# Loads issued by GpSimd instead of SyncE in a row-wise largest-magnitude kernel

## The chip, the cores and the metric

The kernel runs on one core of one Trainium2 chip. A core has several engines with instruction streams of their own: VectorE (DVE), ScalarE (ACT), GpSimd (POOL), TensorE (PE, not used here) and SyncE (SP), which has no arithmetic and issues transfers. Sixteen DMA engines move data between HBM and the on-chip memory SBUF, which has 128 partitions. The metric is the device time of one execution in microseconds. The profile of the kernel before has a span of 625.7 us from its first to its last record, for an execution of 627.43 us.

## The reference

For each row of an 8192 x 8192 matrix of 32-bit floats, the largest absolute value:

```python
def setup_inputs():
    return {"x": np.random.randn(8192, 8192).astype(np.float32)}

def reference(x):
    return np.linalg.norm(x, ord=np.inf, axis=1)
```

Each element is read once and only 8192 numbers are written. There is 268.44 MB to load and 0.03 MB to store.

## The kernel before

The rows are dealt to the 128 partitions so that each partition holds a run of neighbouring rows, 46 in the first group and 18 in the second. A "column" of 8192 elements is then one row of the matrix in every partition, and 64 columns make the whole. Loads are two columns wide (16384 elements, 64 KB in each partition) but for the first two and the last ones. They go into a ring in SBUF that holds three of the wide ones.

```python
GROUPS = [46, 18]
WHOLE = (
    [(8192, ())] * 2 + [(16384, ())] * 29 + [(16384, (3712, 3680)), (8192, (2016, 1984))]
)
LAST = [
    (3920, (1680,)), (1984, (848,)), (1040, (432,)), (576, (240,)), (320, ()), (352, ())
]
RING = 3 * 16384
```

Each entry is the width of a load and, in the inner brackets, what VectorE leaves to ScalarE and GpSimd of its last column: ScalarE makes it absolute, GpSimd takes the maximum. Without inner brackets VectorE reduces it all. The loads:

```python
    def load(pos, w):
        # ... cut: the place in the ring, `at`; the last load has a tile of its own
            buf = ring[:, at : at + w]
        inst = nc.sync.dma_start(out=buf, in_=x_of[first[row]][:, a : a + w]).ins
        # ... cut: for half of the loads, the dependency on the earlier load
        #     of the same place is dropped: the reduce in between orders them
        return buf
```

A load may start when the reduce of what stood in its place is done. The main loop, and the end:

```python
    pos = 0
    for u, (w, g) in enumerate(WHOLE):
        buf = load(pos, w)
        # ... cut
        if whole:
            red = absmax(res[:, row : row + whole], buf[...])     # VectorE
        if g:
            part = single.tile([P, 1 + len(g)], FP32, name=f"part{u}")
            shared(part, buf[:, whole * n_cols :], g)   # VectorE, and ScalarE then GpSimd
            max_pool(res[:, row + whole : row + k], part)         # GpSimd
        # ... cut: an early activation that loads ScalarE's table

    for h, (w, g) in enumerate(LAST[:-1]):
        buf = load(pos, w)
        pos += w
        shared(last[:, n : n + 1 + len(g)], buf, g)
        n += 1 + len(g)

    load(pos, LAST[-1][0])
    absmax(res[:, R - 1 :], last)
    final = nc.sync.dma_start(out=out_of[first[-1]][:, GROUPS[-1] - 1 :], in_=res[:, R - 1 :])
    # ... cut: two earlier stores, issued by ScalarE
```

Line 68 of the kernel is VectorE's reduce, line 75 GpSimd's, line 90 ScalarE's activation, line 108 the load, lines 154 and 159 the stores.

Of the kernel before, what the change touches and what calls it, by code (L numbers as in the profile page):

```python
# [1 line left out]

# [4 lines left out]

P = 128
FP32 = mybir.dt.float32
INT32 = mybir.dt.int32  # L10
MAX = mybir.AluOpType.max
X = mybir.AxisListType.X
ABS = mybir.ActivationFunctionType.Abs
# [16 lines that stand above are left out]
@with_exitstack  # L30
def kernel(
    ctx: ExitStack,
    tc: tile.TileContext,
    x: bass.AP,
    out: bass.AP,
):
    nc = tc.nc
    n_rows, n_cols = x.shape
    R = n_rows // P
    assert R == sum(GROUPS) and n_cols == 8192  # L40
    keep = tc.keep_in_program_order


    first = []
    x_of, out_of = {}, {}
    for k in GROUPS:
        f = len(first)
        x_of[f] = x[f * P : (f + k) * P].rearrange("(p r) m -> p (r m)", r=k)
        out_of[f] = out[f * P : (f + k) * P].rearrange("(p r) -> p r", r=k)
        first += [f] * k  # L50

    single = ctx.enter_context(tc.tile_pool(name="single", bufs=1))

    ring = single.tile([P, RING], FP32)
    res = single.tile([P, R], FP32)

    n_parts = sum(1 + len(g) for w, g in LAST[:-1])
    last = single.tile([P, LAST[-1][0] + n_parts], FP32)

    def not_before(inst, other, why):  # L60
        tc.add_manual_dep(
            inst.ins, other.ins.name,
            mybir.DependencyInfo(mybir.DependencyClass.Sync, mybir.DependencyReason.DATA),
            reason=why,
        )

    def absmax(dst, src):
        return keep(nc.vector.tensor_reduce(  # L68
            out=dst, in_=src, axis=X, op=MAX, apply_absolute_value=True,
        ))  # L70

    def max_pool(dst, src):

        pool = nc.gpsimd
        keep(pool.add_instruction(  # L75
            mybir.InstTensorReduce(
                name=nc.get_next_instruction_name(),
                ins=[pool.lower_ap(src.bitcast(INT32))],
                outs=[pool.lower_ap(dst.bitcast(INT32))],
                op=MAX,  # L80
                axis=X,
            )
        ))

    def shared(part, buf, g):

        a = buf.shape[1] - sum(g)
        red = absmax(part[:, :1], buf[:, :a])
        for i, c in enumerate(g):
            keep(nc.scalar.activation(buf[:, a : a + c], buf[:, a : a + c], ABS))  # L90
            max_pool(part[:, 1 + i : 2 + i], buf[:, a : a + c])
            a += c
        return red

    loads = []

    def load(pos, w):

        row = pos // n_cols
        a = pos - first[row] * n_cols  # L100
        if pos + w == R * n_cols:
            buf = last[:, :w]
        else:
            at = loads[-1][0] + loads[-1][1] if loads else 0
            if at + w > RING:
                at = 0
            buf = ring[:, at : at + w]
        inst = nc.sync.dma_start(out=buf, in_=x_of[first[row]][:, a : a + w]).ins  # L108
        if pos + w < R * n_cols:
            if (len(loads) + 4) % 10 < 5:  # L110


                for b, v, earlier in loads:
                    if b < at + w and at < b + v:
                        tc.declare_no_dep(
                            inst, earlier, reason="ordered by the reduces in between",
                        )
            loads.append((at, w, inst))
        return buf


    pos = 0
    for u, (w, g) in enumerate(WHOLE):
        buf = load(pos, w)
        row, k = pos // n_cols, w // n_cols
        pos += w
        whole = k - 1 if g else k
        if whole:
            red = absmax(
                res[:, row : row + whole],  # L130
                buf[:, : whole * n_cols].rearrange("p (c m) -> p c m", m=n_cols),
            )
        if g:
            part = single.tile([P, 1 + len(g)], FP32, name=f"part{u}")
            shared(part, buf[:, whole * n_cols :], g)
            max_pool(res[:, row + whole : row + k], part)
        if u == 1:

            not_before(
                keep(nc.scalar.activation(res[:, :1], res[:, :1], ABS)),  # L140
                red, "not before the second row is in",
            )


    n = LAST[-1][0]
    for h, (w, g) in enumerate(LAST[:-1]):
        buf = load(pos, w)
        pos += w
        shared(last[:, n : n + 1 + len(g)], buf, g)
        n += 1 + len(g)  # L150

    load(pos, LAST[-1][0])
    absmax(res[:, R - 1 :], last)
    final = nc.sync.dma_start(out=out_of[first[-1]][:, GROUPS[-1] - 1 :], in_=res[:, R - 1 :])


    for f, o in out_of.items():
        k = min(o.shape[1], R - 1 - f)
        early = keep(nc.scalar.dma_start(out=o[:, :k], in_=res[:, f : f + k]))
        tc.add_manual_dep(  # L160
            early.ins, final.ins.name,
            mybir.DependencyInfo(
                mybir.DependencyClass.NoSync, mybir.DependencyReason.SCHED_ONLY
            ),
            reason="takes the later semaphore",
        )


# [1 line left out]
_INS = ['x']  # L170
_OUTS = [((8192,), 'float32')]


# [23 lines left out]
```

## Time and profile before

| What | Value |
|---|---|
| Time, median of 3 runs | 627.56 us (627.45 to 627.61) |
| Mean rate over the span | 429 GB/s |
| VectorE's reduce of 128 x 16384, each of 29 | 17.22 us |
| SyncE's issue of one load | 0.33 to 0.53 us |
| A wide load, issue to landing, median of 30 | 40.8 us |
| First wait of VectorE, for the first load | 12.85 us |

Times in the profile are us from the start of the span. SPq is SyncE's instruction stream, where issuing a load shows; a DMA entry runs from the issue to the landing of the data, so it holds the time in which the load stands behind others in the queue. The chain of waits goes back from the last instruction, at each step to what released it. The groups by line give for VectorE's wide and single reduces together 86.4 us of waiting, all of it for loads.

### The profile page before, as it was taken

How to read it: one execution, taken by the hardware profiler on the slowest of the kernel's cores; microseconds unless marked ns; L12 is line 12 of the kernel's file. 1: busy time of each engine (PE TensorE's matmuls, PEld its weight loads, DVE VectorE, ACT ScalarE, POOL GpSimd, SP SyncE). 2: the span in 40 equal slices, each digit the busy share in tenths (PEclk: the TensorE clock that was granted, in tenths of full speed). 3: DMA queues.
4: the chain of work that ended last, by engine and by line, in shares of the span. 5: the costliest groups of instructions: out<-in, count | busy, mean ns of one | idle time of the engine just before them, and what ended most of it. 6: DMA issues, size and time to landing. Idle time of an engine off the chain costs nothing.

```text
span 625.7 us, 175 instructions
## 1 busy us (share of the span) xinstructions
DVE 536.7 (86%) x40; ACT 15.1 (2%) x10; POOL 14.1 (2%) x14
## 2 busy tenths in 40 slices
DVE  1938988889888899888898888988889888899888
ACT  0000000000000000000000000000000000000044
POOL 0000000000000000000000000000000000000026
DMA  8999999999999999999999999999999999999997
GB/s 369 436 469 402 469 402 469 402 469 402 469 402 457 415 415 457 402 469 402 469 402 469 402 469 402 469 402 453 419 415 457 402 469 402 469 402 469 402 436 304
DMA packets 6048, 268.47 MB, mean 429 GB/s; under 512 B 1056, under 2 KB 1312, under 8 KB 1696
## 3 DMA queue, kind: packets, MB, share of 16 engines
q1 hardware_dynamic: 5760, 268.44, 99.3%
q10 hardware_dynamic: 288, 0.03, 0.0%
HBM read 268.44 MB, written 0.03 MB: 429 GB/s over the span
## 4 chain that ended last, share of the span: by engine, by line
DMA 71%; DVE 28%; SPq 0%; issue 0%; DVEq 0%
DMA ring<-in_x_dram 71%; DVE res L68 28%; DVE last L68 1%; SPq L108 0%; DVEq L68 0%
## 5 line engine op out<-in xcount | busy, mean ns | idle before, releaser
L68 DVE TENSOR_REDUCE res<-ring 128x2 f32<-128x16384 f32 (+1 forms) x32 | 525.4, 16420 | 86.4 <-DMA ring<-in_x_dram 86.4
L90 ACT ACTIVATE ring<-ring 128x3712 f32<-128x3712 f32 (+7 forms) x8 | 13.6, 1719 | 577.2 <-DMA ring<-in_x_dram 573.9
L75 POOL TENSOR_REDUCE part<-ring 128x1 int32<-128x3712 int32 (+3 forms) x4 | 10.1, 2562 | 607.6 <-ACT ring L90 607.6
L68 DVE TENSOR_REDUCE part<-ring 128x1 f32<-128x800 f32 (+1 forms) x2 | 5.5, 2748 | 0.1
L68 DVE TENSOR_REDUCE last<-ring 128x1 f32<-128x2240 f32 (+4 forms) x5 | 5.3, 1115 | 0.1
L75 POOL TENSOR_REDUCE last<-ring 128x1 int32<-128x1680 int32 (+3 forms) x4 | 3.4, 855 | 0.6 <-ACT ring L90 0.4
L140 ACT ACT_TABLE_LOAD x1 | 1.3, 1283 | 0.7 <-PEq L181 0.7
L140 ACT ACTIVATE res<-res 128x1 f32<-128x1 f32 x1 | 0.2, 203 | 29.3 <-DVE res L68 29.3
L68 DVE TENSOR_REDUCE res<-last 128x1 f32<-128x361 f32 x1 | 0.5, 529 | 0.1
L75 POOL TENSOR_REDUCE res<-part 128x1 int32<-128x3 int32 x2 | 0.4, 198 | 0.1
L181 POOL MEMSET const-float32-0.0<- 128x1 f32 x1 | 0.1, 99 | 0.2 <-issue 0.2
L181 POOL MEMSET const-bfloat16-1.0<- 128x1 bf16 x1 | 0.1, 102 | 0.0
L181 POOL MEMSET const-uint8-127<- 128x1 uint8 x1 | 0.1, 101 | 0.0
L181 POOL MEMSET const-float32-1.0<- 128x1 f32 x1 | 0.1, 99 | 0.0
## 6 DMA issues: line engine op xcount, KB each, us to landing
ring<-in_x_dram SPq DMA_DIRECT2D x3, 4096.0 KB, 21.4
ring<-in_x_dram SPq DMA_DIRECT2D x1, 1960.0 KB, 35.4
ring<-in_x_dram SPq DMA_DIRECT2D x1, 992.0 KB, 37.4
ring<-in_x_dram SPq DMA_DIRECT2D x1, 520.0 KB, 38.2
ring<-in_x_dram SPq DMA_DIRECT2D x30, 40.8
ring<-in_x_dram SPq DMA_DIRECT2D x1, 288.0 KB, 38.4
last<-in_x_dram SPq DMA_DIRECT2D x1, 176.0 KB, 38.3
ring<-in_x_dram SPq DMA_DIRECT2D x1, 160.0 KB, 38.3
```

Source lines behind the costliest of these rows:

```text
L68: return keep(nc.vector.tensor_reduce(out=dst, in_=src, axis=X, op=MAX, apply_absolute_value=True,))
L75: keep(pool.add_instruction(mybir.InstTensorReduce(name=nc.get_next_instruction_name(), ins=[pool.lower_ap(src.bitcast(INT32))], outs=[poo ...
L90: keep(nc.scalar.activation(buf[:, a : a + c], buf[:, a : a + c], ABS))
L140: keep(nc.scalar.activation(res[:, :1], res[:, :1], ABS)),
L181: nc = _bacc.Bacc("TRN2", target_bir_lowering=False, num_devices=1)
```

## The change

GpSimd issues every load instead of SyncE. GpSimd also has reduces of its own at the end of the kernel, and its stream is kept in program order, so a load that stood behind one of those reduces would come late. Therefore, as soon as the first shared column comes, all remaining loads are issued, and GpSimd's reduces follow them. The last store stays on SyncE. What is loaded, where to and in what order doesn't change, nor do the reduces. It tries the other way of starting a transfer: SyncE has its descriptors (the lists of what goes where) made by hardware, GpSimd makes them in software.

```diff
-        inst = nc.sync.dma_start(out=buf, in_=x_of[first[row]][:, a : a + w]).ins
+        inst = keep(nc.gpsimd.dma_start(out=buf, in_=x_of[first[row]][:, a : a + w])).ins
...
+    widths = [w for w, _ in WHOLE + LAST]
+    bufs = []
+
+    def load_up_to(n):
+        while len(bufs) < n:
+            bufs.append(load(sum(widths[: len(bufs)]), widths[len(bufs)]))
+
     pos = 0
     for u, (w, g) in enumerate(WHOLE):
-        buf = load(pos, w)
+        load_up_to(len(widths) if g else u + 1)
+        buf = bufs[u]
...
-    for h, (w, g) in enumerate(LAST[:-1]):
-        buf = load(pos, w)
-        pos += w
+    for buf, (w, g) in zip(bufs[len(WHOLE) :], LAST[:-1]):
         shared(last[:, n : n + 1 + len(g)], buf, g)
         n += 1 + len(g)
 
-    load(pos, LAST[-1][0])
     absmax(res[:, R - 1 :], last)
```

## The prediction

> **What bounds the kernel now.** I read the busy table first, then the DMA queues, the chain that ended last, a table of stretches, and a timeline of the end. By the page VectorE (DVE) is busy for 86% of the span and the DMA queue of the loads for over 99%:
>
> ```profile
> DVE 536.7 (86%) x40; ACT 15.1 (2%) x10; POOL 14.1 (2%) x14
> ...
> q1 hardware_dynamic: 5760, 268.44, 99.3%
> ```
>
> The second line is queue, packets, MB and share of sixteen DMA engines. The input is 8192 x 8192 x 4 bytes = 268.44 MB, so every byte is moved once. 39 loads and the last store, which shares SP's queue, make 5760 packets, 144 each: one for each of the 128 partition rows, and 16 short ones. A row of a two-column load is 16384 x 4 = 65,536 bytes, and it goes as one packet.
>
> The chain of waits shows how a round goes (start, length, what):
>
> ```profile
> 59.16 0.02 issue
> 59.17 40.78 DMA ring<-in_x_dram
> 99.95 0.02 issue
> 99.97 17.23 DVE res L68
> ...
> 564.39 17.23 DVE res L68
> 581.62 0.02 issue
> 581.64 0.33 SPq L108
> 581.97 0.05 issue
> 582.02 35.44 DMA ring<-in_x_dram
> 617.45 0.02 issue
> 617.47 5.30 DVE last L68 x5
> ```
>
> A reduce ends at 59.16, its third of the ring is free, the next load is issued at once and lands 40.78 us later. From 59.16 to 581.62 the chain makes nine such rounds of three loads each: 27 loads in 522.46 us, 19.35 us a load, and 8.389 MB / 19.35 us = 433.5 GB/s. A chain that alternates DMA and DVE looks like a latency loop. But of the 40.78 us only 19.35 are the load's own transfer; the other 21.43 are the loads queued ahead of it, and its issue and latency lie beside them. The table of stretches confirms that the queue doesn't run dry (stretch, length, busy DVE, ACT, POOL, clock, DMA share, GB/s):
>
> ```profile
> 59.17:117.22 58.05, 51.66 (x3) 0.00 (x0) 0.00 (x0) 1.00 1.00 434
> 117.22:291.37 174.15, 154.97 (x9) 0.00 (x0) 0.00 (x0) 1.00 1.00 434
> 291.37:581.64 290.27, 258.30 (x15) 0.00 (x0) 0.00 (x0) 1.00 1.00 433
> ```
>
> So the middle is bound by the rate of the DMA engines. VectorE needs 17.22 us for what takes 19.35 to load and isn't the bound. Only the ends are latency. SyncE (SP) issues the first load at 0.74 us and VectorE begins on it at 12.85, 12.1 us later, of which 4.194 MB / 433.5 GB/s = 9.7 are transfer and 2.4 fixed. The end, in the timeline:
>
> ```profile
> 562.29 22.05 SPq L108 DMA_DIRECT2D ring<-in_x_dram  x7
> ...
> 584.38 0.43 SPq L108 DMA_DIRECT2D last<-in_x_dram  x1
> ...
> 606.55 6.48 POOL L75 TENSOR_REDUCE part<-ring 128x1 int32<-128x3712 int32 x2 [606.11 <-ACT ring L90]
> ...
> 622.86 0.53 DVE L68 TENSOR_REDUCE res<-last 128x1 f32<-128x361 f32 x1
> 623.41 0.35 SPq L154 DMA_DIRECT2D out_dram<-res  x1
> ```
>
> The last load is issued at 584.38 and lands 38.3 us later by the page's table of DMA issues, at 622.7, when VectorE is just done with the pieces before it; the last reduce and the last store make the remaining 3 us of the 625.7 us span. GpSimd (POOL) begins its first reduce only at 606.55.
>
> **What the Trainium skill says.** First, "DMA: Bandwidth & Descriptors", section "Issuing engines are not separate DMA queues": loads started by any engine run on the same 16 DMA engines, and the choice of issuer saves only sequencer time. The trace has one issuer of loads, so it can't show this yet; the 433.5 GB/s agrees with the 435 GB/s that the same page's "Specifications" gives as the fabric's ceiling. Second, that table puts the first byte at about 1 us on GpSimd's software path and 0.6 us on SP's hardware path. No run here shows the first of these; the 2.4 us fixed share of the first load holds more than the first byte. Third, that page's "The descriptor swizzle" says that the software path writes 9 read and 9 write descriptors per DMA engine for a 1 MiB transfer to 128 partitions: 8 rows and a completion. The trace of before has 144 = 16 x 9 packets a load, the same structure, but from the hardware path. Fourth, "SBUF — State Buffer", section "Who interferes with whom": a DMA from GpSimd can be starved while VectorE holds the port pair they share, but tensor_reduce on trn2 never takes it. VectorE does nothing but tensor_reduce here, for 86% of the time, so much hangs on that; the trace of before can't confirm it.
>
> **The change part by part.**
> Removed: 39 issues of loads on SP, of 0.33 to 0.53 us each, and the waits ahead of them. In the middle they lie beside 21 us of queued transfers. Worth 0.
> Added: 39 loads on GpSimd, whose cores write the descriptors in software. The trace has no duration for this; from the skill's first-byte figures I take about 1 us a load as an estimate. A load in the middle may come later by 21.43 - 2.4 = 19.0 us (queued time less fixed latency) before the DMA engines run dry. One or two us are thus free. Worth 0 for all loads but the first and those of the end.
> The first load: nothing lies ahead of it, and the DMA engines are busy from then to the end, so its delay goes in full into the time. The two first-byte figures differ by 0.4 us; writing 128 rows' descriptors in software before all 16 engines have work may add as much again. I take +1.0. The second load, behind 9.7 us of the first's transfer, is covered.
> The burst at the end: seven small and middle loads become free at once at 581.64, when one reduce frees their third of the ring. SP issues them in 3.2 us (581.64 to 584.38 + 0.43). GpSimd at 1 to 2 us each takes 7 to 14 us and is done by 596 at the latest. The transfer ahead of them lasts to about 603 (VectorE begins its last 8192-column reduce at 603.10), and GpSimd's own first reduce begins at 606.55. Both have over 7 us to spare, which is what issuing all loads ahead of its own work gives. Worth 0.
> The rate: rows, packets, DMA engines and order stay as they are if a 64 KB row stays one descriptor. 0 as the centre, with a tail to the slow side.
> The end of the program: another queue with eight more semaphores to wait for; I take +0.3 as a guess.
> The sum: 627.56 + 0 + 1.0 + 0 + 0 + 0.3 = 628.9, said as 629.0.
>
> **The rivals.**
> The software path cuts rows into shorter descriptors. A 64 KB packet of one engine now takes 19.35 / 8 = 2.42 us, for which 27.2 GB/s (the ceiling's sixteenth) would give 2.41. If a piece cost some 3 to 4 ns more (the skill, "DMA: Bandwidth & Descriptors", section "Why small descriptors are slow (HBM only)", has 3 cycles per packet) then halves would cost 4 ns in 2.42 us, 0.2% or 1 us; pieces of 4 KB would cost 15 x 3.5 = 53 ns, 2.2%, or 13.5 us in all: 642. Nothing in the profile speaks for it, and the 9 descriptors of the skill speak against, though for rows of 8 KB only.
> VectorE starves the descriptor writing. If each load waited for the end of a running reduce, that is up to 17.22 us, plus about 1 us of writing. This is just inside the 19.0 us of slack, so the middle would hardly move, but the seven loads of the end would be issued late and the DMA engines would have gaps: 5 to 20 us, 633 to 648. The skill speaks against.
> Uneven engines: [...] if one of the 16 runs 1% slower all loads end with it: 620 us x 1% = +6, 634. A queue of two loads doesn't level a lasting difference. It is possible that fetching is instead smoother; the ceiling is 0.4% above the measured rate, so at most -2.4 us: 626.5.
> A first call of GpSimd's descriptor code could cost some us more at the start, each going straight into the time.
>
> **How the range follows.** The time is the transfer of 268.44 MB at 433.5 GB/s, 619.2 us, plus about 8 us of ends. Faster by 2% means 615.0, less than the transfer alone: 1%. Slower by 2% means 640.1: it takes the small pieces or real starvation, 11% together. The rest is 88%. Low end 626.5 (smoother fetching, start as before), high end 638 (an uneven engine, or a slow start with halves).
>
> **What would show it.** The DMA queue's line should read software instead of hardware, with about 144 packets a load; more packets means the first rival. The stretches of the middle should still read 433 or 434 GB/s with a share of 1.00, and a three-load round 58.05 us; if less, look for starvation (GpSimd's issues end when reduces end) or an uneven engine. VectorE's first reduce should begin at 13.5 to 14.5 instead of 12.85, and everything after it be later by as much. GpSimd's burst should begin near 582 and end before 597, and its first reduce come at about 607.5. The prediction is wrong if the middle's round differs from 58.05 by more than 0.3 us (nine rounds make 3 us of it), or the first reduce begins after 16.

## The result and the profile after

| | before | after |
|---|---|---|
| Time, median | 627.50 us (627.44 to 627.61, 4 runs) | 629.95 us (629.80 to 630.04, 4 runs) |
| Ratio | | 1.0039, 95% interval 1.0021 to 1.0056 |
| Span of the profiled execution | 625.7 us | 628.0 us |

The changed kernel takes 2.45 us more; the prediction was 629.0 with a range of 626.5 to 638. The page of after has these lines for the busy time and the queue of the loads:

```profile
DVE 536.6 (85%) x40; ACT 15.0 (2%) x10; POOL 34.8 (6%) x53
...
q0 software_dynamic: 5376, 268.44, 98.9%
```

The loads are now in a queue of software kind with the same bytes, and GpSimd has 20.7 us more to do, which is 39 loads of about 0.53 us. The packets are 5376, where 39 times 144 would be 5616; this comes back below. The chain of waits of after (start, length, what):

```profile
60.15 0.28 issue
60.43 40.52 DMA ring<-in_x_dram
100.95 0.03 issue
100.97 17.23 DVE res L68
...
565.38 17.23 DVE res L68
582.61 0.28 issue
582.89 0.52 POOL ring L108
583.41 35.51 DMA ring<-in_x_dram
618.92 0.02 issue
618.94 5.23 DVE last L68 x5
```

From 60.15 to 582.61 are again 522.46 us for nine rounds, the very number of before. The issue now begins 0.28 us after the reduce that frees the ring, against 0.02 on SyncE, and the chain absorbs it: the load lands 40.52 us after its issue instead of 40.78. Stretches of after (stretch, length, busy DVE, ACT, POOL, clock, DMA share, GB/s):

```profile
60.60:118.60 58.00, 51.66 (x3) 0.00 (x0) 1.53 (x4) 1.00 1.00 434
291.37:581.64 290.27, 258.32 (x16) 0.00 (x0) 7.92 (x15) 1.00 1.00 433
```

So nothing was lost in the middle. The timeline of after shows both ends:

```profile
1.25 2.25 POOL L108 DMA_DIRECT2D ring<-in_x_dram  x4 [0.80 <-PEq L198]
13.85 8.69 DVE L68 TENSOR_REDUCE res<-ring 128x1 f32<-128x8192 f32 x1 [13.85 <-DMA ring<-in_x_dram]
...
586.03 0.54 POOL L108 DMA_DIRECT2D last<-in_x_dram  x1
...
607.54 6.47 POOL L75 TENSOR_REDUCE part<-ring 128x1 int32<-128x3712 int32 x2 [20.98 <-ACT ring L90]
...
624.26 0.53 DVE L68 TENSOR_REDUCE res<-last 128x1 f32<-128x361 f32 x1
624.82 0.38 SPq L160 DMA_DIRECT2D out_dram<-res  x1
```

Beside the times of before, the loss splits in three:

| Term | before | after | grows by |
|---|---|---|---|
| VectorE begins on the first load | 12.85 | 13.85 | 1.00 |
| Last store issued, less the line above | 623.41 - 12.85 = 610.56 | 624.82 - 13.85 = 610.97 | 0.41 |
| End of the span, less the last store's issue | 625.7 - 623.41 = 2.3 | 628.0 - 624.82 = 3.2 | 0.9 |

I call them the start, tail and closing terms. They sum to the 2.3 us by which the spans differ. The closing term shows among the synchronising instructions of the program's last line. These are its drains in before (first fence) and in after (second; count, ns min/median/max, first and last start in us); DRAIN is the records' name for an instruction that every engine carries out there:

```profile
L192 POOLq DRAIN  x3: 34/83/484, 622.3 to 625.4; - x3
L192 SPq DRAIN  x3: 7/7/7, 624.9 to 625.2; - x3
```

```profile
L198 POOLq DRAIN  x3: 40/95/3694, 623.6 to 627.8; - x3
L198 SPq DRAIN  x3: 7/7/7, 626.5 to 627.5; - x3
```

Before, GpSimd's longest drain takes 0.48 us and is over at 622.8, two us ahead of SyncE, which waits for the last store. After, it takes 3.69 us from 623.6 and ends at 627.3, 0.8 us after SyncE has come to its own at 626.5. GpSimd has become the last to finish.

### The profile page after: what moved, and what is told of

It reads as the page before. It is cut to its first block, busy times and chain, and to the rows that moved or that the text cites. A ratio compares the mean times of both kernels' runs of the same rounds, so it can differ in the third digit from the quotient of the medians.

```text
span 628.0 us, 176 instructions
## 1 busy us (share of the span) xinstructions
DVE 536.6 (85%) x40; ACT 15.0 (2%) x10; POOL 34.8 (6%) x53
## 3 DMA queue, kind: packets, MB, share of 16 engines
q0 software_dynamic: 5376, 268.44, 98.9%
## 4 chain that ended last, share of the span: by engine, by line
DMA 76%; DVE 23%; issue 0%; POOL 0%; DVEq 0%; PEldq 0%
DMA ring<-in_x_dram 76%; DVE res L68 22%; DVE last L68 1%; POOL ring L108 0%; DVEq L68 0%; PEldq L198 0%
## 5 line engine op out<-in xcount | busy, mean ns | idle before, releaser
L108 POOL DMA_DIRECT2D ring<-in_x_dram x38 | 20.2, 533 | 565.4 <-DVE res L68 564.6
## 6 DMA issues: line engine op xcount, KB each, us to landing
ring<-in_x_dram POOLq DMA_DIRECT2D x1, 288.0 KB, 38.1
```

What stands on the lines that cost most here:

```text
L108: inst = keep(nc.gpsimd.dma_start(out=buf, in_=x_of[first[row]][:, a : a + w])).ins
```

## The experiments

The theory: the cost lies at the ends (1.0 + 0.4 + 0.9), none of it in the loads of the middle. Its first rival spreads it, 2.45 / 39 = 0.06 us for each load. Others concern what makes the drain long. Unless said otherwise the base is the changed kernel. Ratios are to the kernel before, run on the same chip.

**First load on SyncE.**

```diff
+        eng = nc.sync if len(loads) < 1 else nc.gpsimd
-        inst = keep(nc.gpsimd.dma_start(...)).ins
+        inst = keep(eng.dma_start(...)).ins
```

> First load on SyncE, the other 38 on GpSimd. Theory (the 2.45 us lie at the ends: start 1.0, tail 0.5, closing 0.9): the DMA engines start at 1.7 us in the span as in the kernel before, the start term goes away and nothing else does, so about 629.0, 1.0 under the changed kernel. Rival (each software load costs a little, 2.45 / 39 = 0.06 us): 629.9, no visible gain.

Measured: 628.92 us, ratio 1.0023 (1.0014 to 1.0033), 1.03 less than the changed kernel. One load of 39 on the other engine takes away 1.0 us, sixteen times the rival's share for one load. The start term is shown. Its timeline:

```profile
0.74 0.37 SPq L109 DMA_DIRECT2D ring<-in_x_dram  x1
1.25 1.73 POOL L109 DMA_DIRECT2D ring<-in_x_dram  x3 [0.80 <-PEq L199]
20.14 17.28 DVE L68 TENSOR_REDUCE res<-ring 128x1 f32<-128x8192 f32 x2 [20.14 <-DMA ring<-in_x_dram]
```

The first load and GpSimd's next ones now share the DMA engines, so VectorE begins only at 20.14, and that costs nothing. The first data packet begins at 1.73, as in the kernel before (1.74), and at 2.64 in the changed kernel: what counts is when the DMA engines start, not when the first reduce does.

**First load alone on GpSimd.** The condition turned round: `len(loads) >= 1` on SyncE.

> First load alone on GpSimd, the other 38 on SyncE, which starts its first at 0.74 us. The DMA engines start as early as before, so no start term; the tail is SyncE's, so no tail term. Theory A of the closing term (any software load makes GpSimd's closing drain long, whenever it was): 627.5 + 0.9 = 628.4, drain over 3 us. Theory B (the drain waits for what the software queue still holds, or for the last landing): 627.5, drain about 0.5 us. The rival of 0.06 us a load: 627.6.

Measured: 627.60 us, ratio 1.0001 (0.9993 to 1.0010). Theory A, by which any software load makes the drain long, falls; its longest drain:

```profile
L199 POOLq DRAIN  x3: 39/94/573, 622.3 to 625.5; - x3
```

It is 0.57 us, 0.09 above that of the kernel before. One software load costs nothing that shows in the time.

**GpSimd's four small reduces at the end left out.** The results of GpSimd's four last reduces, of 1680, 848, 432 and 240 columns, are not computed; zeros written at the start stand in their place.

```diff
-            max_pool(part[:, 1 + i : 2 + i], buf[:, a : a + c])
+            if pool:      # False for the pieces of LAST
+                max_pool(part[:, 1 + i : 2 + i], buf[:, a : a + c])
```

> The changed kernel without GpSimd's four reduces of the small last pieces (left out; their places hold zeros), so that GpSimd's last instruction ends some 4 us earlier, near 619.7 instead of 624. Theory A1 (the closing drain lasts a fixed 3.7 us from its start): it ends near 623.4, ahead of the last store, and the closing term of 0.9 vanishes: 629.0 or 629.1. Theory B1 (the drain ends some 3.4 us after the last load has landed): 629.95, unchanged.

Measured: 629.01 us, ratio 1.0025 (1.0015 to 1.0035). The 0.9 us are gone, as theory A1 has it, though nothing of the loads changed. But the drain isn't what A1 says:

```profile
L201 POOLq DRAIN  x3: 40/95/6240, 619.5 to 627.2; - x3
L201 SPq DRAIN  x3: 7/7/7, 626.6 to 626.9; - x3
```

It begins earlier by 4.1 us and lasts 6.24 instead of 3.69, until 625.7. The last load is issued at 586.03 and lands 38.1 us later, at 624.1. So the drain has no fixed length. That it waited here for loads in flight fits these times but isn't shown, and why it ended some 1.6 us after the last landing stays open. It ended ahead of SyncE's at 626.6, and that made the closing term vanish.

**All loads on ScalarE.** This is the hardware path again, on another engine with work of its own; the first four loads are issued ahead of ScalarE's early activation.

```diff
+        inst = keep(nc.scalar.dma_start(...)).ins
+        load_up_to(len(widths) if g else max(4, u + 1))
```

> All loads on ScalarE, which has the hardware path as SyncE, the first four ahead of its table load and its first activation. If the cost belongs to the software path: about 627.5 to 627.9 (only a later start of ScalarE's stream could cost), no long drain, 144 packets a load. If it belongs to leaving SyncE for an engine with work of its own: about 629.9.

Measured: 627.95 us, ratio 1.0008 (1.0000 to 1.0016). Start and closing terms are absent (first reduce at 12.94, longest GpSimd drain 0.48 us), so both belong to the software path and not to leaving SyncE. But the last store is issued at 623.97, and 623.97 - 12.94 = 611.03 against 610.56: a tail term of 0.5 us is here too. So that one doesn't belong to the software path alone.

**The first 20 loads on GpSimd, the rest on SyncE, and the reverse.** `len(loads) >= 20` on SyncE, and `len(loads) < 20`. By now the drains suggested a price for each software load.

> The first 20 loads on GpSimd, the last 19 on SyncE. The closing drains so far were 3.69 us with 39 software loads, 3.61 with 38, 0.57 with 1, 0.48 with none. Theory (the drain costs 0.082 us for each software load of the whole program, whenever it was): 0.48 + 20 x 0.082 = 2.13 us, which ends before the last store is through and costs nothing; the start term of 1.0 stays: 628.4 to 628.8, with up to 0.3 for the change of queue. Rival (the drain depends on what was loaded lately): 0.5 us, same time. Rival (any larger number gives 3.7): 629.3.

> The first 20 loads on SyncE, the last 19 on GpSimd. Theory (0.082 us for each software load): drain 0.48 + 19 x 0.082 = 2.05 us, no closing term, no start term, only the tail: 627.6 to 628.1. Rival (what was loaded lately sets the drain): 3.7 us and 628.5 to 628.9.

Measured: GpSimd first 630.85 us, ratio 1.0052 (1.0039 to 1.0064); SyncE first 627.87 us, ratio 1.0007 (0.9998 to 1.0015). The drains, first in GpSimd first, then in SyncE first:

```profile
L199 POOLq DRAIN  x3: 40/108/2142, 625.4 to 628.9; - x3
```

```profile
L199 POOLq DRAIN  x3: 40/108/2059, 622.3 to 625.7; - x3
```

Both are as long as their number of software loads says, whether these were early or late. The drains of all numbers of software loads that were run, where GpSimd's own reduces end the work (ns):

| Software loads | 0 | 1 | 19 | 20 | 38 | 39 |
|---|---|---|---|---|---|---|
| Longest drain | 484 | 573 | 2059 | 2142 | 3612 | 3694 |
| 484 + 82.3 for each | 484 | 566 | 2048 | 2130 | 3611 | 3694 |

This settles the closing term: the drain costs 0.082 us for each software load of the whole program, after GpSimd's last reduce, and shows in the time only for what reaches beyond the last store. With 20 loads it is over before SyncE comes to its own drain; with 39 it costs 0.8 us. The rival of a cost for each load was right in the kind of thing and wrong in where it is paid. All loads have 128 rows, so these runs can't tell a price for a load from one for its rows.

SyncE first still takes 0.41 us more than the kernel before, and their runs don't overlap (627.79 to 627.98 against 627.36 to 627.54). Its last store is issued at 623.40, as before, but the span ends 2.5 us after that instead of 2.3, and this isn't explained.

The time of GpSimd first missed its expectation by 2 us. In its timeline VectorE waits once for 21.49 us where the queues change, and in SyncE first 19.07 us (first and second fence; both views end at 500 us):

```profile
391.15 119.98 DVE L68 TENSOR_REDUCE res<-ring 128x2 f32<-128x16384 f32 x7 [21.49 <-DMA ring<-in_x_dram]
```

```profile
387.81 119.98 DVE L68 TENSOR_REDUCE res<-ring 128x2 f32<-128x16384 f32 x7 [19.07 <-DMA ring<-in_x_dram]
```

There, two queues share the DMA engines for a while, two loads land together, and then eight reduces stand one behind the other. This is so in both kernels. The difference of 2.4 us between the two waits is about the size of the miss; that it is the cause isn't shown. Why one order of queues loses this and the other doesn't stays open, and the runs of GpSimd first scatter (629.57 to 631.73).

**An issue delayed by 11 us in the middle.** Unneeded reduces of a scratch tile stand ahead of 21 loads, tied to the reduce that frees the ring.

```diff
+            if 6 <= len(bufs) < 27:
+                for i in range(4):
+                    busy = max_pool(scratch[:, 3200:], scratch[:, :3200])
+                    if i == 0:
+                        not_before(busy, reds[len(bufs) - 3], ...)
             bufs.append(load(...))
```

> Changed kernel; ahead of each of 21 loads in the middle GpSimd does four reduces of 128 x 3200 (about 2.84 us each by the 3.28 us of 128 x 3712), begun only when the reduce that frees the ring is done: each of these loads is issued about 11.4 us later. Theory (19 us of queued transfers cover an issue's delay): no change, 629.9 to 630.2. Rival (the chain of DMA and VectorE is a latency loop, delays add): 7 rounds x 11.4 = +80 us, 710.

Measured: 630.15 us, ratio 1.0044 (1.0030 to 1.0057), as the changed kernel. In the timeline the issue comes 11.7 us after the end of the reduce (304.49 against 275.56 + 17.22 = 292.78), and VectorE's next wait is still 2.14:

```profile
275.56 17.22 DVE L71 TENSOR_REDUCE res<-ring 128x2 f32<-128x16384 f32 x1 [2.13 <-DMA ring<-in_x_dram]
292.93 11.62 POOL L78 TENSOR_REDUCE scratch<-scratch 128x1 int32<-128x3200 int32 x4 [7.25 <-DVE res L71]
...
304.49 0.55 POOL L111 DMA_DIRECT2D ring<-in_x_dram  x1
...
333.62 17.22 DVE L71 TENSOR_REDUCE res<-ring 128x2 f32<-128x16384 f32 x1 [2.14 <-DMA ring<-in_x_dram]
```

The latency loop that the chain seems to show isn't there. One or two us of software per load couldn't be seen in the middle of this kernel.

**Delayed by 23 us, on GpSimd.** `range(8)` in the same edit.

> The same with eight reduces, about 22.7 us. Theory: a round of three loads is then no longer 58.05 us of transfer but 17.2 (reduce) + 0.3 + 22.7 + 0.5 (issue) + 2.4 (fixed) + 19.35 (own transfer) = 62.5, so 7 rounds x 4.4 = +31 us, about 661, with gaps in the DMA engines' work. Rival (latency loop): 7 x 22.7 = +159, 789.

Measured: 723.85 us, ratio 1.1536 (1.1520 to 1.1552). Neither expectation was right, as the experiment had a bound of its own:

```profile
293.36 0.55 POOL L111 DMA_DIRECT2D ring<-in_x_dram  x1
293.92 23.34 POOL L78 TENSOR_REDUCE scratch<-scratch 128x1 int32<-128x3200 int32 x8
...
317.20 0.55 POOL L111 DMA_DIRECT2D ring<-in_x_dram  x1
```

GpSimd has no gap: an issue comes each 317.20 - 293.36 = 23.84 us, and 21 x (23.84 - 19.35) = 94 us, which is 723.85 - 629.95. It tested GpSimd's throughput and not the slack. The next pair puts the delay on two engines.

**Delayed by 23 and by 17 us, on two engines.** Base is the kernel before. A chain of 15 (or 11) operations of 128 x 1600 stands ahead of each of the 21 loads, on ScalarE for odd and GpSimd for even ones, and SyncE's load waits for the last of them.

```diff
+        for i in range(15):                  # 11 in the second kernel
+            if u % 2: busy = keep(nc.scalar.activation(scratch[1]..., ABS))
+            else:     busy = max_pool(scratch[0]...)
+            if i == 0: not_before(busy, reds[u - 3], ...)
-        buf = load(pos, w)
+        buf = load(pos, w, delay(u) if 6 <= u < 27 else None)
```

> The kernel before, loads on SyncE, but ahead of each of 21 loads in the middle stands a chain of 15 operations of 128 x 1600 (about 1.55 us each, 23 us), on GpSimd for even and ScalarE for odd loads, so that no engine has more than 23 us of work in two loads' 38.7 us; a chain begins when the reduce that frees the ring is done. Theory (an issue may come 19 us later, no more): a round is 17.2 + 0.2 + 23 + 0.35 + 2.4 + 19.35 = 62.5 instead of 58.05, so 7 x 4.4 = +31 us, 650 to 668. Rival (latency loop): 7 x 23 = +161, 789. Rival (the slack is larger, as more than one load is queued): 627.5.

> The same with 11 operations, about 17 us: inside the 19 us. Theory: a round would be 56.5 by latency, less than the 58.05 of transfer, so no change: 627.3 to 628.5. Rival (latency loop): 7 x 17 = +119, 747.

Measured: 664.09 us, ratio 1.0595 (1.0570 to 1.0619), and 630.87 us, ratio 1.0051 (1.0034 to 1.0067). Chain of waits of the kernel with 23 us, around one load:

```profile
290.59 17.23 DVE res L72
307.86 0.04 issue
307.90 1.54 ACT scratch L104
...
331.41 21.84 DMA ring<-in_x_dram
353.25 0.02 issue
353.27 17.23 DVE res L72
```

Now the loop is real: reduce, delay, and a landing after 21.84 us, which is 19.35 of transfer and 2.5 of latency, so nothing was left queued ahead of it. This round takes 353.27 - 290.59 = 62.68 us, where 62.5 was expected. The seven rounds with delayed loads, from 99.86 to 542.67 us, take 442.81 us, which is 36.5 more than seven of 58.05 and explains the time. With 17 us the delay should have been hidden and cost 3.4. The issues there come 17.3 to 17.6 us after the reduces, VectorE's waits scatter from 2.10 to 2.95 us, and the seven rounds take 58.15 to 58.88 us, so single loads already come late. The slack is thus somewhat less than the 19 us of the prediction: 11.7 us are free, 17.3 to 17.6 cost 0.5%.

## Why the prediction was right

- **The bound.** Right. Nine rounds take 522.46 us in both kernels. Issues 11.7 us after the release change nothing; delays of 23 us on two engines change it by the loop's arithmetic.
- **Issues in the middle, worth 0.** Right. The estimate of 1 us for a load was high: GpSimd's record of an issue is 0.53 us, after 0.28 from the release.
- **The first load, +1.0.** Right in size, 1.00 in the trace and 1.03 by putting that one load back, but half of it by luck. GpSimd's first issue begins at 1.25 and SyncE's at 0.74, so 0.5 us are GpSimd coming to its first load later, which the prediction didn't have. From the start of the issue to the first data packet it is 2.64 - 1.25 = 1.39 us on GpSimd and 1.74 - 0.74 = 1.00 on SyncE. This difference of 0.4 us agrees with that of the two figures, 1 and 0.6 us, of the Trainium skill's page "DMA: Bandwidth & Descriptors", section "Specifications". Of the further 0.4 us that the prediction added for the writing of 128 rows' descriptors, 0.1 is left.
- **The burst, worth 0.** Right: seven issues from 582.89 to 586.57, and GpSimd's own first reduce at 607.54, one us after that of before, like everything else.
- **The rate, 0 as the centre.** Right for the middle. For the tail the term missed 0.4 us, treated below.
- **The end of the program, +0.3 as a guess.** This term was mis-sized: 0.9, of which 0.8 is GpSimd's drain. The prediction had more semaphores in mind; the runs show 0.082 us for each software load, paid after GpSimd's last reduce. With the tail's 0.4 these are the 1.0 us between 629.0 and 629.95.
- **Rival, shorter descriptors.** Fell, and the opposite holds. Wide rows stay whole: 3840 packets of 65,536 bytes in both traces (30 loads x 128), with a median of 2.42 us. Short rows are put together, see the last section.
- **Rival, VectorE starves the descriptor writing.** Fell: GpSimd's issues are 0.53 us beside a VectorE that reduces for 85% of the time, and 38 of 39 lie between 0.527 and 0.541 (the first takes 0.685). This agrees with the Trainium skill's "SBUF — State Buffer", section "Who interferes with whom", on tensor_reduce.
- **Rival, uneven engines.** Not as a lower rate of one engine: the middle moves 433 to 434 GB/s in both kernels. But the tail term could be a constant lag of some engines. The starts and lengths of the DMA packets give the spreads below; the records don't name the engine, so the first 16 and the last 16 data packets are taken as one of each:

| Kernel | First packets begin within | Last packets end within | Last store, less first packet |
|---|---|---|---|
| before | 0.58 us | 0.17 us | 621.67 us |
| after | 0.99 us | 0.58 us | 622.18 us |
| all on ScalarE | 0.98 us | 0.64 us | 622.22 us |
| small reduces left out | 0.80 us | 0.72 us | 622.38 us |
| delayed by 11 us | 0.85 us | 0.79 us | 622.27 us |
| first load on SyncE | 0.32 us | 0.49 us | 621.91 us |
| first load alone on GpSimd | 0.91 us | 0.20 us | 621.67 us |
| first 20 loads on SyncE | 0.63 us | 0.30 us | 621.65 us |

If each engine moves the same bytes without a gap, one that starts 0.5 us late can't catch up, and the last pieces wait for it. The first five kernels, with one issuer of all loads, fit this. The last three, with two issuers, speak against it: the first load on SyncE starts closest together and still has a tail of 0.24 us, and the first load alone on GpSimd starts 0.91 us apart and has none. The tail goes with the spread at the end; what makes that spread stays open. It isn't the software path's alone, as all loads on ScalarE have it, and GpSimd's 19 loads at the end bring none when SyncE has the first 20.

No run beat the kernel before, and the terms say why: in the middle the DMA engines are at their rate with either path, and what the software path changes at the ends are costs.

## What to carry to other kernels

In a chain of waits that alternates transfer and compute, take the transfer's own time and the fixed latency out of "issue to landing" before calling it a latency loop; the rest is queue, and most of that was free for a slower issuer here (11.7 of some 19 us; 17.3 cost 0.5%). Where the queue never ran dry, the change of issuer cost only at the first packet and in the last microseconds. Look at the closing drain of an engine that issues by software: this program pays there for all of its 39 loads at once, and what ends before the last store costs nothing.

## What the runs showed of the hardware

The software path puts short rows into common packets. These are the packet counts of before (first) and after (second):

```profile
DMA packets 6048, 268.47 MB, mean 429 GB/s; under 512 B 1056, under 2 KB 1312, under 8 KB 1696
```

```profile
DMA packets 5810, 268.48 MB, mean 428 GB/s; under 512 B 1057, under 2 KB 1057, under 8 KB 1457
```

The 256 packets between 512 B and 2 KB, rows of 320 and 352 columns (1280 and 1408 bytes), are gone. The trace's sizes in their place are 5120 = 4 x 1280, 4224 = 3 x 1408 with a rest of 2816 = 2 x 1408, and 4608 = 2 x 2304 for the rows of 576 columns, while rows of 4160 bytes and more stay single. So rows are joined up to about 4 KB, or until the engine's eight rows are used up: three rows of 1280 bytes (3840) get a fourth, while a row of 4160 stays alone. That makes 15 packets fewer for each of 16 engines, 240 in all, and 5616 - 240 = 5376. No gain in time was found for it.

The other two were not expected either: the drain's 0.082 us for each software load, and a first reduce that may begin 14.5 us later (27.38 instead of 12.85, with the first load alone on GpSimd) at no cost, since the DMA engines had begun on time (first data packet at 1.74 us in both).
